# Sums of x begun in an earlier block, cached keys transposed later in half pairs, bias rows built beside the pair of values

## The chip, the cores and the metric

The kernel runs on one NeuronCore of a Trainium2 chip. The core has TensorE (PE, matrix multiply), VectorE (DVE), ScalarE (ACT), GpSimd (POOL) and SyncE (SP), which here only issues DMA transfers. Each engine works through its own instructions in the order in which they are written; an instruction waits until the semaphores it needs are set, and everything behind it on the same engine waits with it. TensorE writes to PSUM, and ACT and DVE copy the results from there to SBUF.

The metric is the device time of one execution in microseconds. Before the change the runs gave 1001.48, 997.56 and 995.86 us, a median of 997.56.

## The reference, cut to what matters

One layer of a streaming encoder runs on 1024 new prompt frames and 64 sample frames, with 512 cached frames for the samples.

```python
def project(x, norm_w, w_in, q_norm_w, k_norm_w):
    h = rms_norm(x, norm_w) @ w_in                      # (T, 1024) @ (1024, 6144)
    sb_q, sb_k, sb_v, sb_z, cb_q, cb_k, cb_v, cb_z, g_sb, g_cb = jnp.split(h, SPLIT_POINTS, axis=-1)
    ...
    cb_q = rms_norm(cb_q.reshape(lead + (N_HEADS_CB, HEAD_DIM)), q_norm_w)
    cb_k = rms_norm(cb_k.reshape(lead + (N_HEADS_CB, HEAD_DIM)), k_norm_w)
    ...
k_all = jnp.concatenate([cache_sb_k[l], sk2], axis=1)   # 512 cached keys + 64 new ones
o_sb2 = stick_breaking(sq2, k_all, v_all, s_qpos, sb_s_kpos)
kb = jnp.concatenate([cache_cb_k[l], ck2], axis=1)
o_cb2 = band_attention(cq2, kb, vb, s_qpos, cb_s_kpos, rel_bias[l])
```

The band attention adds a bias that depends on the clipped distance of query and key (`rel_bias`, 8 heads of 257 numbers). Then both branches are gated, projected, merged and added to x.

## The kernel before

Every float32 product is made of float32r parts: a value is split into a high part (ACT copies it, rounded) and a low part (value minus high part, on DVE or POOL), and hi·hi, lo·hi and hi·lo are summed in PSUM. On top of that stands a Strassen-like scheme with seven products in place of eight for the large projections; it needs sums of quarters of x and of quarters of the weights.

The order of the work on each engine is written out by hand: the program is emitted in loops, and what is emitted first is executed first on its engine. The stages that the change touches are these, in order:

- **Normalise and transpose x** (block 0 of the next loop carries it).
- **Plain blocks.** The loop over `i in range(nb)` with `nb = 6` (`NB = [1024, 1280, 2560, 2816, 2048, 2304]`) makes 256 columns of the projection for nine token tiles `ti` each. Blocks 0 and 1 are values of branch A and have no norm; blocks 2 and 3 are keys of branch B, blocks 4 and 5 its queries. In blocks 2 to 5 each tile needs a norm per head (`evac_nat`, `norm_nat`: a square on ACT, a reduction and two products on DVE, a power on POOL), and up to three tiles later `post_nat` transposes it on PE (tile `pk`, one PSUM buffer) and splits it (`hl`, L359 on ACT and L360 on DVE).
- Beside block 1 the cached keys are transposed: `cache_load` fetches a whole cache (`ck`, 1 MB), and `cache_pair` transposes 128 columns of it on PE into `pc`, splits them into `hc` (L379 on ACT, L380 on DVE; one buffer) and stores them to DRAM for the attention. The bias rows are built there too: `load_rb` fetches `rel_bias` to all partitions, `make_rb` negates and lays out a row for each head (`rx`, L249 and L250 on DVE) and stores it.
- Beside blocks 2 to 5 `make_t` forms the sums of x (`d`, L169 to L177 on DVE; `t0` to `t3`, ACT and L158 on DVE) in 17 pieces (`tjobs`), one at every second tile.
- **The pair of values** (`OPV`, L654 on PE) makes the values of branch B by the seven-product scheme.
- **The paired stage** (the loop over `pairs`, L832 on PE) makes 14 pairs of 128 columns, seven steps `s` each; a step is 24 matmuls. Step `n = 7*i + s` begins by preparing weights five steps ahead (`prep`, `presum`, `load_raw`), then `step()` emits what earlier steps left for later: stores of finished parts (`hl`) and, for key pairs, `out`, which transposes the part on PE (`kf`, `u`, `s` into `acc`, two PSUM buffers) and stores it (`ko`, `kos`). The first four pairs are keys and queries of branch A, and their stores are the most numerous.
- Attention, output projections and the last product follow; the change leaves them as they are.

Nearly all DMAs of these stages are issued by SP, in program order, stores and loads in one row. A store that waits for DVE holds the loads behind it.

Of the kernel before, what the change touches and what calls it, by code (L numbers as in the profile page):

```python
# [32 lines left out]
def hybrid_step_kernel(ctx: ExitStack, tc: tile.TileContext, x_prompt, x_sample, c_sbk, c_sbv, c_cbk, c_cbv,  # L33
# [15 lines left out]
    def rdma(out, in_):  # L49
        out, in_ = (a if isinstance(a, bass.AP) else a[:] for a in (out, in_))  # L50
        SP.dma_start(out.bitcast(F32), in_.bitcast(F32))
# [149 lines left out]
    with ExitStack() as ph:  # L201
# [37 lines left out]

        rbs = {}  # L240

        def load_rb():
            rbs[0] = p1.tile([128, 8, 257], F32, name="ck", bufs=3)
            SP.dma_start(rbs[0], rel_bias[0:1].to_broadcast([128, 8, 257]))

        def make_rb(h):
            rb = rbs[0]
            rx = p1.tile([128, 768], F32, name="rx", bufs=3)
            V.tensor_scalar(rx[:, 0:512], rb[:, h, 256:257].to_broadcast([128, 512]), -1.0, None, op0=OP.mult)  # L249
            V.tensor_scalar(rx[:, 512:768], rb[:, h, 255::-1], -1.0, None, op0=OP.mult)  # L250
            SP.dma_start(d_rb[h], rx)

        def rsqrt(dst, src, scale, n):
# [111 lines left out]
                    if t == 3:  # L365
                        rdma(dst[p0 + j][:, :, NP:T], h[:, j, :, 512:576])

        def cache_load(b):
            src = c_sbk if b == "sb" else c_cbk
            ck = p1.tile([128, 4, 512], F32, name="ck", bufs=3)  # L370
            SP.dma_start(ck, src.rearrange("(t p) c -> p t c", p=128))
            cks[b] = ck

        def cache_pair(b, p):
            pt = psK.tile([128, 4, 128], F32, name="pc")
            for t in range(4):
                TE.transpose(pt[:, t], cks[b][:, t, p * 128:(p + 1) * 128], ident)
            h = p1.tile([128, 2, 512], F32R, name="hc", bufs=1)
            A.activation(h[:, 0], pt[:].rearrange("p t c -> p (t c)"), AF.Copy)  # L379
            V.tensor_tensor(out=h[:, 1], in0=pt[:].rearrange("p t c -> p (t c)"), in1=h[:, 0].bitcast(F32),  # L380
                            op=OP.subtract)
            rdma(d_cT[b][p], h)

        raws, blk, sums = {}, {}, {}
        def load_raw(n):
            if n >= 2 * len(pairs):
# [32 lines left out]
        def prep(n):  # L419

            i, s = divmod(n, 7)
            if i >= len(pairs):
                return
            a, b = slice(0, 128), slice(128, 256)
            r1, r2 = raws[2 * i], raws[2 * i + 1] if s else None
            if s == 0:
                src = r1[:, :, a]
            elif s == 3:
                src = r2[:, :, a]
            elif s == 5:  # L430
# [8 lines left out]
            A.activation(t[:, 0], src, AF.Copy)  # L439
            G.tensor_tensor(out=t[:, 1], in0=src, in1=t[:, 0].bitcast(F32), op=OP.subtract)  # L440
            blk[n] = t
            if s == 6:
                load_raw(2 * i + 4)
# [44 lines left out]
        def v_sum(n):  # L488
            x, y, op, pool, name, bufs = {
                2: ((0, 1), (1, 1), OP.add, natx, "wlox", 2), 1: (2, (0, 0), OP.subtract, natx, "wlox", 2),  # L490
                4: ((0, 0), (0, 1), OP.subtract, natx, "whix", 2), 6: ((1, 0), 1, OP.subtract, None, "t6", 1)}[n]
            d = vraw[n] = (pool or pv2).tile([128, 4, 256], F32, name=name, bufs=bufs)
            V.tensor_tensor(out=d, in0=vraw[x], in1=vraw[y], op=op)

        def prep_v(q):
# [24 lines left out]
        for i in range(nb):  # L520
            for ti, t in enumerate(TO):
# [34 lines left out]
                if ti in (3, 6) and i > 0 or ti in (6, 7) and i == 0:  # L556
# [4 lines left out]
                        load_nat(i + 2, h)  # L561
                    else:
                        load_v_raw(*((0, 0), (1, 0), (0, 1), (1, 1))[2 * (i + 2 - nb) + h])
                if (i, ti) in ((0, 5), (0, 8)):
                    cache_load("sb" if ti == 5 else "cb")
                if i == 1 and ti < 8:
                    if ti == 0:
                        load_rb()
                    cache_pair("sb" if ti < 4 else "cb", ti % 4)
                if 10 <= 9 * i + ti < 18:  # L570
                    make_rb(9 * i + ti - 10)
                if (i, ti) == (1, 0):
                    psTx.close()
                if (i, ti) == (1, 8):
                    p1x.close()
                    tp = sx.enter_context(tc.tile_pool(name="tp", bufs=1))
                    pad(tp, 64)
                    tms = [[tp.tile([128, 4, HF], F32R, name=f"t{n}{s}") for s in "hl"] for n in range(4)]
                    tqx = ExitStack()
                    tq = tqx.enter_context(tc.tile_pool(name="tq", bufs=3))  # L580
                    tjobs = iter(make_t(tms, tq))
                if i > 1 and (i + ti) % 2:
                    next(tjobs, None)
                if (i, ti) == (nb - 1, 5):
                    prep_v(0)
                if (i, ti) == (nb - 1, 8):
                    v_sum(2)
                if (i, ti) in ((1, 1), (1, 5)):
                    for s in range(2):
                        h = ti // 4  # L590
# [39 lines left out]
        for q, s in enumerate(OPV):  # L630
# [14 lines left out]
            for c in range(2):  # L645
# [58 lines left out]

    with ExitStack() as ph:
        up = ph.enter_context(tc.tile_pool(name="a2u", bufs=3, side="right"))
        psB = ph.enter_context(tc.tile_pool(name="a2p", bufs=1, space=PS))
        LEAD, HB = 5, 4
        later = []

        def soon(n, f):
# [99 lines left out]
        for i in range(len(pairs)):  # L811
            bank, s1, u2, u3 = {}, {}, {}, {}
            for s in range(7):
# [941 lines left out]
```

## Time and profile before

| what | value |
|---|---|
| median of the three runs | 997.56 us |
| the profiled execution | 1000.77 us, of which the span is 999.0 us |
| PE busy | 964.0 us (96%) |
| DVE / ACT / POOL busy | 606.2 / 475.2 / 403.9 us |
| PE waits for DVE at the transposes of normed tiles (`pk`) | 14.9 us in 9 waits |
| PE waits for DVE at the transposes of cached keys (`pc`) | 10.6 us in 3 waits |
| plain block 1 | 42.78 to 84.84 us |
| plain blocks 2 to 5 | 84.84 to about 208 us |
| pair of values | about 208 to 257 us |
| paired stage | 257.56 to about 550 us |

The page's busy shares say which engine is the bound over the whole span. For a change that moves work between stages, a table by stage says more: the busy time of each engine in a stretch, the clock that TensorE was granted there (1.00 is full speed), and the DMA share. The list of waits tells who waited for whom; the rows of SP in order of time tell when a transfer was issued, and a row with `x3` is three instructions merged, its length from the first's start to the last's end, waits between them included.

### The profile page before, as it was taken

The page shows a single profiled execution, that of the slowest core. Times are in us where ns is not written, and L with a number is a line of the kernel's source. Part 1 is how long each engine was busy: PE and PEld are TensorE (multiplying, and loading weights), DVE is VectorE, ACT ScalarE, POOL GpSimd, SP SyncE. Part 2 cuts the span into 40 slices and gives each one's busy share as a digit, 9 for nine tenths or more (in the row PEclk, how much of TensorE's full clock was granted, in tenths as well). Part 3 has the DMA queues.
Part 4 walks back from the last instruction along what each step waited for, and adds up shares of the span by engine and source line. Part 5 has one row for each costly group of instructions (what it writes and reads, how often), then busy time and mean ns, then how long its engine had stood idle before and what let it go on. Part 6 is the DMA issues. An engine that isn't in the chain of part 4 may idle for free.

```text
span 999.0 us, 20386 instructions
## 1 busy us (share of the span) xinstructions
PE 964.0 (96%) x7591; PEld 915.0 (92%) x7591; DVE 606.2 (61%) x1185; ACT 475.2 (48%) x1046; POOL 403.9 (40%) x395
## 2 busy tenths in 40 slices
PE   8959789889999999999999999999999999999998
PEld 8959789889999999999999988788888889999998
DVE  6524899863545455553332267788668766389735
ACT  6513344342344343343333266677787776455220
POOL 3212665554545447655643211001341111596641
PEclk9989899999999999999999999999999999999999
DMA  6876234224565655556632697778799951862642
GB/s 220 264 253 238 81 103 148 98 93 134 164 178 160 199 163 182 163 162 190 186 109 78 186 278 209 204 200 233 213 265 268 247 152 56 249 209 81 200 137 84
DMA packets 173192, 175.76 MB, mean 176 GB/s; under 512 B 30553, under 2 KB 157405, under 8 KB 172966
## 3 DMA queue, kind: packets, MB, share of 16 engines
q1 hardware_dynamic: 161542, 159.45, 54.4%
q10 hardware_dynamic: 8736, 8.33, 2.6%
q0 software_dynamic: 2816, 6.69, 2.1%
q8 instruction: 60, 0.98, 0.4%
q14 instruction: 38, 0.31, 0.1%
HBM read 112.42 MB, written 62.00 MB: 175 GB/s over the span
## 4 chain that ended last, share of the span: by engine, by line
PE 82%; DVE 8%; DMA 4%; ACT 3%; issue 1%; POOL 1%; SPq 0%; ACTq 0%; DVEq 0%; POOLq 0%
PE b L832 29%; PE o L1349 7%; PE acc L519 7%; PE z L1257 7%; PE pt L1310 7%; PE b L1669 6%; PE acc L1108 5%; PE acc L1001 5%; PE b L1150 4%; PE v L654 3%; DMA d_csbT<-hc 2%; DVE qn L335 1%; DMA d_ccbT<-hc 1%; PE pt L283 1%; PE pk L355 1%
## 5 line engine op out<-in xcount | busy, mean ns | idle before, releaser
L1279 DVE TENSOR_TENSOR_SCAN be<-be,imp 128x128 f32<-128x128 f32 (+7 forms) x64 | 83.4, 1344 | 8.1 <-ACT be L1260 7.9
L1310 PE MATMUL pt<-ident,be 128*128 128x128 f32 (+1 forms) x568 | 87.7, 278 | 0.6 <-ACT wT L1319 0.2
L1257 PE MATMUL z<-ks,sq 128*128 128x320 f32 (+5 forms) x384 | 87.5, 338 | 0.0
L1310 PEld LDWEIGHTS pt<-ident,be 128*128 128x128 f32 (+1 forms) x568 | 65.7, 140 | 13.0 <-issue 4.6
L1319 ACT ACTIVATE wT<-pt 128x512 f32<-128x512 f32 (+3 forms) x123 | 57.0, 497 | 42.8 <-PE pt L1310 42.7
L840 DVE TENSOR_TENSOR u<-b,s 128x256 f32<-128x256 f32 (+1 forms) x56 | 24.1, 439 | 70.4 <-PE b L832 65.7
L1257 PEld LDWEIGHTS z<-ks,sq 128*128 128x128 f32 x384 | 63.6, 190 | 1.7
L1349 PE MATMUL o<-wT,vp 128*64 128x256 f32 (+1 forms) x608 | 64.2, 356 | 0.0
L1349 PEld LDWEIGHTS o<-wT,vp 128*64 128x64 f32 x608 | 40.3, 136 | 23.6 <-issue 7.5
L519 PE MATMUL acc<-whi,xa 128*128 128x256 f32 x192 | 55.6, 309 | 0.2 <-ACT xa L291 0.2
L1282 ACT ACTIVATE be<-be,sm 128x640 f32<-128x640 f32 (+5 forms) x68 | 47.2, 694 | 17.2 <-DVE sm L1281 17.1
L905 POOL DMA_DIRECT2D d_osb<-zt x20 | 10.8, 541 | 102.1 <-DVE zt L1358 63.2
L124 POOL TENSOR_TENSOR wlo<-wraw,whi 128x1024 fp32r<-128x1024 f32 x13 | 32.0, 2458 | 49.3 <-ACT whi L117 46.1
L519 PE MATMUL acc<-whi,xm 128*128 128x256 f32 x192 | 51.9, 290 | 0.0
L519 PE MATMUL acc<-wlo,xa 128*128 128x256 f32 x192 | 51.8, 289 | 0.0
L519 PE MATMUL acc<-whix,xm 128*128 128x256 f32 x192 | 50.6, 283 | 0.0
L519 PE MATMUL acc<-whix,xb 128*128 128x256 f32 x192 | 50.4, 282 | 0.0
L519 PE MATMUL acc<-wlox,xm 128*128 128x256 f32 x192 | 50.3, 282 | 0.0
L440 POOL TENSOR_TENSOR whix<-ws,whix 128x512 fp32r<-128x512 f32 x28 | 36.9, 1317 | 32.5 <-ACT whix L439 28.2
L1270 ACT ACTIVATE be<-be,sm 128x640 f32<-128x640 f32 (+5 forms) x68 | 47.3, 696 | 5.0 <-DVE sm L1262 4.5
L1260 ACT ACTIVATE be<-z 128x384 f32<-128x384 f32 (+6 forms) x104 | 47.9, 515 | 3.2 <-PE z L1257 2.4
L440 POOL TENSOR_TENSOR wlo<-ws,wlo 128x512 fp32r<-128x512 f32 x28 | 39.5, 1412 | 18.1 <-ACT wlo L439 17.9
(387 smaller groups left out, 3334.7 us busy)
## 6 DMA issues: line engine op xcount, KB each, us to landing
wraw<-in_w_in_dram SPq DMA_DIRECT2D x31, 512.0 KB, 4.1
wrawx<-in_w_in_dram SPq DMA_DIRECT2D x16, 512.0 KB, 4.8
sq<-d_qsbT SPq DMA_DIRECT2D x32, 192.0 KB, 6.1
sq<-d_qcbT SPq DMA_DIRECT2D x32, 192.0 KB, 5.2
xt<-in_x_prompt_dram SPq DMA_DIRECT2D x8, 512.0 KB, 6.5
d_kcbT<-hl SPq DMA_DIRECT2D x8, 512.0 KB
d_qcbT<-hl SPq DMA_DIRECT2D x8, 512.0 KB, 4.4
d_ksbT<-hl SPq DMA_DIRECT2D x16, 256.0 KB, 3.1
```

The costliest lines, as they stand in the source:

```text
L440: G.tensor_tensor(out=t[:, 1], in0=src, in1=t[:, 0].bitcast(F32), op=OP.subtract)
L519: TE.matmul(ps, x, w, start=first, stop=last)
L832: TE.matmul(ps[:, :m], w[:, hl_, k], right[s](x)[:, k, a:b], start=s < 3 and k == 0 and e == 0, stop=k == 3 and e == 2, skip_group_check=s ...
L1001: TE.matmul(ps[:, :b - a], w[:, k], xk(x, k)[:, a:b], start=k == 0 and n == 0, stop=k == KT - 1 and n == 2)
L1108: TE.matmul(ps[:, :e - a], w[:, p, cw], g[:, a:e], start=m % 12 == 0, stop=m % 12 == 11)
L1257: TE.matmul(z[:, :m], s[:, e, q0:q0 + 128], ks[:, h, o + x:o + y], start=(e, h) == parts[0], stop=(e, h) == parts[-1])
L1260: A.activation(be[:r, x:y], z[:r, :m], AF.Sigmoid, scale=-0.125)
L1279: V.tensor_tensor_scan(be[:r, n - 1::-1], be[:r, n - 1::-1], im[:, ::-1], 0.0, op0=OP.mult, op1=OP.max)
L1310: TE.transpose(pt[:kr, x, :r], be[:r, kb * 128:kb * 128 + kr], ident[:r, :r])
L1319: A.activation(w[:, sl:sl + m, q0:q0 + r], pt[:, :m, :r], AF.Copy)
L1349: TE.matmul(o[hd * 64:hd * 64 + 64, c0:c1], vv[:kr, kb, hd * 64:hd * 64 + 64], wT[b, p, j, hd, s // 4][:kr, s % 4, c0:c1] if j < 4 else wT ...
L1669: TE.matmul(ps[:, t], left[s](xs_, k)[:, ts_], wt_[:, k], start=s < 3 and t == k == e == 0, stop=k == 3 and e == 2, skip_group_check=s > 2 ...
```

## The change

Four things move.

1. `make_t` begins in block 1 instead of block 2: a piece at each tile from (1, 1) on, eight in block 1, and then one at every fourth tile instead of every second. The pool of block 0 is closed at (1, 0), and the copies of sample columns that the sums read are made at the end of block 0.
2. `cache_load` and `cache_pair` leave blocks 0 and 1. In the paired stage, steps 2 to 33, an even step loads a half pair (256 tokens by 128 columns, 128 KB, one buffer `ck`) and the odd step after it transposes it (two transposes into `acc`, split into `hc`, stored in the next `step()`): 16 loads and 16 parts.
3. The bias rows leave blocks 0 to 2: one row a head is loaded (`rb`) after product 2 of the pair of values, and `make_rb` is called beside products 3 to 5.
4. After the plain blocks the remaining `post_nat` are called one at a time in place of two, over products 0 to 2. `v_sum(6)` uses another buffer, and the low part of weight block 1 is made on DVE in place of POOL.

On DVE, at block 1, where a split of weights (L124) and the fold of the sample tile (L299) come first, the rows before are those of the cached keys and the bias rows:

```order
L124 TENSOR_TENSOR wlox<-wrawx,whix 128x1024
L299 TENSOR_TENSOR fl<-acc,fl 64x256
L380 TENSOR_TENSOR hc<-pc,hc 128x512
L596 TENSOR_SCALAR wqk<-wqk 128x64
L380 TENSOR_TENSOR hc<-pc,hc 128x512
L249 TENSOR_SCALAR rx<-ck 128x512
L250 TENSOR_SCALAR rx<-ck 128x256
```

The same place in the changed kernel, still on DVE:

```order
L124 TENSOR_TENSOR wlox<-wrawx,whix 128x1024
L299 TENSOR_TENSOR fl<-acc,fl 64x256
L572 TENSOR_SCALAR wqk<-wqk 128x64
L169 TENSOR_TENSOR d<-xa 128x544
L170 TENSOR_TENSOR d<-d,xm 128x544
L171 TENSOR_TENSOR d<-d,xm 128x544
L176 TENSOR_TENSOR d<-xm,d 128x544
L177 TENSOR_TENSOR d<-d,xb 128x544
L158 TENSOR_TENSOR t0l<-d,t0h 128x544
```

The sums of x stand where the cached keys and bias rows stood.

On SP, at the first key pair of the paired stage, before: raw weights (`wraw`, `wrawx`), stores of key parts (`hl`) and of the transposed outputs (`ko`, `kos`).

```order
L395 DMA wraw<-in_w_in_dram 128x4x256 x2
L51 DMA d_ksbT_70<-hl 256x1x256 x2
L51 DMA d_ksbT_70<-hl 256x1x32
L395 DMA wrawx<-in_w_in_dram 128x4x256
L764 DMA out_dram<-ko 128x2x128
L761 DMA out_dram<-kos 32x128
L764 DMA out_dram<-ko 128x2x128
L51 DMA d_ksbT_71<-hl 256x1x256 x2
L51 DMA d_ksbT_71<-hl 256x1x32
```

And SP at the same place after, with loads of half pairs (`ck`) and stores of the split keys (`hc`) between them:

```order
L379 DMA wraw<-in_w_in_dram 128x4x256 x2
L696 DMA ck<-in_cache_sb_k_dram 128x2x128
L51 DMA d_csbT_78<-hc 256x1x256
L51 DMA d_ksbT_70<-hl 256x1x256 x2
L51 DMA d_ksbT_70<-hl 256x1x32
L696 DMA ck<-in_cache_sb_k_dram 128x2x128
L379 DMA wrawx<-in_w_in_dram 128x4x256
L763 DMA out_dram<-ko 128x2x128
L760 DMA out_dram<-kos 32x128
L763 DMA out_dram<-ko 128x2x128
L51 DMA d_ksbT_71<-hl 256x1x256 x2
L51 DMA d_ksbT_71<-hl 256x1x32
```

Each load of a half pair stands behind the stores that its step emits.

On PE, at the end of step 4 and the begin of step 5 of the paired stage (`t2` and `t3` are sums of x, `kf` a finished key part), before:

```order
L832 MATMUL b_3332<-t2l,whix 128x288
L832 MATMUL b_3332<-t2h,whix 128x288
L756 MATMUL acc<-ident,kf 128x128 x4
L758 MATMUL acc<-ident,kf 32x128
L832 MATMUL b_3317<-t3h,whi 128x256
```

And PE there after:

```order
L833 MATMUL b_3273<-t2l,whix 128x288
L833 MATMUL b_3273<-t2h,whix 128x288
L755 MATMUL acc<-ident,kf 128x128 x4
L757 MATMUL acc<-ident,kf 32x128
L702 MATMUL acc<-ident,ck 128x128 x2
L833 MATMUL b_3258<-t3h,whi 128x256
```

Two transposes of a half pair now stand ahead of the step's matmuls.

The diff, cut to its core:

```diff
-        def load_rb():
-            rbs[0] = p1.tile([128, 8, 257], F32, name="ck", bufs=3)
-            SP.dma_start(rbs[0], rel_bias[0:1].to_broadcast([128, 8, 257]))
+        def load_rb(h):
+            rbs[h] = pv2.tile([128, 257], F32, name="rb", bufs=3)
+            SP.dma_start(rbs[h], rel_bias[0:1, h:h + 1].to_broadcast([128, 1, 257]).rearrange("p o n -> p (o n)"))
 
         def make_rb(h):
-            rb = rbs[0]
-            rx = p1.tile([128, 768], F32, name="rx", bufs=3)
...
+            rb = rbs.pop(h)
+            rx = pv2.tile([128, 768], F32, name="rx", bufs=2)
...
-        def cache_load(b):
...
-        def cache_pair(b, p):
...
-            G.tensor_tensor(out=t[:, 1], in0=src, in1=t[:, 0].bitcast(F32), op=OP.subtract)
+            (V if n == 1 else G).tensor_tensor(out=t[:, 1], in0=src, in1=t[:, 0].bitcast(F32), op=OP.subtract)
...
-                if (i, ti) in ((0, 5), (0, 8)):
-                    cache_load("sb" if ti == 5 else "cb")
-                if i == 1 and ti < 8:
-                    if ti == 0:
-                        load_rb()
-                    cache_pair("sb" if ti < 4 else "cb", ti % 4)
-                if 10 <= 9 * i + ti < 18:
-                    make_rb(9 * i + ti - 10)
                 if (i, ti) == (1, 0):
                     psTx.close()
-                if (i, ti) == (1, 8):
+                if (i, ti) == (1, 0):
                     p1x.close()
...
                     tjobs = iter(make_t(tms, tq))
-                if i > 1 and (i + ti) % 2:
+                elif i == 1 or i > 1 and (9 * i + ti) % 4 == 0:
                     next(tjobs, None)
...
-                if (i, ti) in ((1, 1), (1, 5)):
+                if (i, ti) in ((0, 7), (0, 8)):
...
-                if q < 2:
-                    for _ in range(2):
-                        if pend and (q or c):
-                            post_nat(*pend.pop(0))
+                if q < 3 and pend and (q or c):
+                    post_nat(*pend.pop(0))
+                for h in {(3, 0): (0,), (3, 1): (1, 2), (4, 0): (3,), (4, 1): (4, 5), (5, 0): (6,), (5, 1): (7,)}.get((q, c), ()):
+                    make_rb(h)
+                    if h + 3 < 8:
+                        load_rb(h + 3)
...
-            if q == 1:
+            if q == 2:
                 assert not pend
...
             if q == 2:
+                for h in range(3):
+                    load_rb(h)
                 v_sum(4)
...
+        cjobs = [(b, p, h) for b in ("sb", "cb") for p in range(NPAIR) for h in range(2)]
+        cks = {}
+
+        def cache_load(b, p, h):
+            cks[b, p, h] = cq.tile([128, 2, 128], F32, name="ck")
+            src = (c_sbk if b == "sb" else c_cbk)[256 * h:256 * h + 256, p * 128:(p + 1) * 128]
+            SP.dma_start(cks[b, p, h], src.rearrange("(t p) c -> p t c", p=128))
+
+        def cache_part(b, p, h):
+            ck = cks.pop((b, p, h))
+            pt = psF.tile([128, 512], F32, name="acc")[:, 0:256]
+            for t in range(2):
+                TE.transpose(pt[:, t * 128:(t + 1) * 128], ck[:, t], ident)
+            hc = cq.tile([128, 2, 256], F32R, name="hc")
+            A.activation(hc[:, 0], pt, AF.Copy)
+            V.tensor_tensor(out=hc[:, 1], in0=pt, in1=hc[:, 0].bitcast(F32), op=OP.subtract)
+            soon(0, lambda: rdma(d_cT[b][p][:, :, 256 * h:256 * h + 256], hc))
...
                 step()
+                if 2 <= n < 2 + 2 * len(cjobs):
+                    (cache_part if n % 2 else cache_load)(*cjobs[(n - 2) // 2])
```

More of the change, by code (lines that the diff above doesn't have):

```diff
@@ L240, in hybrid_step_kernel @@
         rbs = {}
-        def load_rb():
-            rbs[0] = p1.tile([128, 8, 257], F32, name="ck", bufs=3)
-            SP.dma_start(rbs[0], rel_bias[0:1].to_broadcast([128, 8, 257]))
+        def load_rb(h):
+            rbs[h] = pv2.tile([128, 257], F32, name="rb", bufs=3)
+            SP.dma_start(rbs[h], rel_bias[0:1, h:h + 1].to_broadcast([128, 1, 257]).rearrange("p o n -> p (o n)"))
         def make_rb(h):
-            rb = rbs[0]
-            rx = p1.tile([128, 768], F32, name="rx", bufs=3)
-            V.tensor_scalar(rx[:, 0:512], rb[:, h, 256:257].to_broadcast([128, 512]), -1.0, None, op0=OP.mult)
-            V.tensor_scalar(rx[:, 512:768], rb[:, h, 255::-1], -1.0, None, op0=OP.mult)
+            rb = rbs.pop(h)
+            rx = pv2.tile([128, 768], F32, name="rx", bufs=2)
+            V.tensor_scalar(rx[:, 0:512], rb[:, 256:257].to_broadcast([128, 512]), -1.0, None, op0=OP.mult)
+            V.tensor_scalar(rx[:, 512:768], rb[:, 255::-1], -1.0, None, op0=OP.mult)
             SP.dma_start(d_rb[h], rx)
@@ L366, in post_nat @@
                         rdma(dst[p0 + j][:, :, NP:T], h[:, j, :, 512:576])
-        def cache_load(b):
[L369 to L372, printed above, removed]
-        def cache_pair(b, p):
[L375 to L382, printed above, removed]
         raws, blk, sums = {}, {}, {}
@@ L490, in v_sum @@
                 2: ((0, 1), (1, 1), OP.add, natx, "wlox", 2), 1: (2, (0, 0), OP.subtract, natx, "wlox", 2),
-                4: ((0, 0), (0, 1), OP.subtract, natx, "whix", 2), 6: ((1, 0), 1, OP.subtract, None, "t6", 1)}[n]
-            d = vraw[n] = (pool or pv2).tile([128, 4, 256], F32, name=name, bufs=bufs)
+                4: ((0, 0), (0, 1), OP.subtract, natx, "whix", 2), 6: ((1, 0), 1, OP.subtract, natx, "wlox", 2)}[n]
+            d = vraw[n] = pool.tile([128, 4, 256], F32, name=name, bufs=bufs)
             V.tensor_tensor(out=d, in0=vraw[x], in1=vraw[y], op=op)
@@ L587, in hybrid_step_kernel @@
                     v_sum(2)
-                if (i, ti) in ((1, 1), (1, 5)):
+                if (i, ti) in ((0, 7), (0, 8)):
                     for s in range(2):
-                        h = ti // 4
+                        h = ti - 7
                         for c in range(2):
@@ L706, in hybrid_step_kernel @@
         up = ph.enter_context(tc.tile_pool(name="a2u", bufs=3, side="right"))
+        cq = ph.enter_context(tc.tile_pool(name="cq", bufs=1))
         psB = ph.enter_context(tc.tile_pool(name="a2p", bufs=1, space=PS))
         LEAD, HB = 5, 4
+        cjobs = [(b, p, h) for b in ("sb", "cb") for p in range(NPAIR) for h in range(2)]
[13 more added lines that the diff above has]
+            soon(0, lambda: rdma(d_cT[b][p][:, :, 256 * h:256 * h + 256], hc))
         later = []
```

## The prediction

> **What bounds the kernel now.** I read the page's busy shares first, then a table by stage.
>
> ```profile
> PE 964.0 (96%) x7591; PEld 915.0 (92%) x7591; DVE 606.2 (61%) x1185; ACT 475.2 (48%) x1046; POOL 403.9 (40%) x395
> ```
> ```profile
> 42.78:84.84 42.06, 31.46 (x242) 30.86 (x241) 9.97 (x22) 9.73 (x19) 5.99 (x6) 0.88 0.74 251
> 84.84:116.44 31.60, 27.93 (x220) 27.54 (x219) 20.95 (x40) 11.12 (x28) 15.63 (x17) 0.89 0.33 119
> 116.44:148.07 31.63, 27.16 (x229) 26.16 (x228) 29.20 (x55) 12.94 (x34) 18.57 (x20) 1.00 0.39 127
> 148.07:177.08 29.01, 28.23 (x228) 27.76 (x228) 26.77 (x53) 13.46 (x35) 18.50 (x20) 0.94 0.42 142
> 177.08:208.20 31.12, 28.34 (x230) 27.93 (x228) 27.00 (x53) 11.98 (x33) 16.90 (x21) 0.95 0.32 106
> 208.20:224.60 16.40, 13.19 (x99) 12.71 (x97) 8.67 (x14) 6.05 (x12) 7.70 (x6) 0.90 0.26 89
> ...
> 257.56:299.14 41.58, 41.58 (x332) 41.04 (x333) 21.25 (x40) 17.94 (x45) 23.25 (x16) 1.00 0.57 171
> ```
>
> The columns are stretch, length, busy time of PE, PE's weight loads, DVE, ACT and POOL, then granted clock, DMA share and GB/s. The first five stretches are plain blocks 1 to 5, the sixth the begin of the pair of values. PE idles there, and its clock is not full. In blocks 3 to 5 DVE is busy 92, 92 and 87%. In the paired stage (last row) PE has no gap and full clock: whatever is put on its path there is paid in full. The waits and the chain of waits say who holds PE in the plain blocks:
>
> ```profile
> PE pk L355 <- DVE hl L360: 14.9, 9, 3.7
> PE pc L377 <- DVE hc L380: 10.6, 3, 7.8
> ```
> ```profile
> 48.88 8.85 DMA d_csbT<-hc
> 57.83 0.61 ACT hc L379
> 58.46 0.70 DVE hc L380
> 59.18 2.64 DMA d_csbT<-hc
> ...
> 110.77 2.74 PE acc L519 x24
> ...
> 113.51 0.23 PE pk L355 x2
> ```
>
> In block 1 the one `hc` buffer makes a chain: store, ACT, DVE, store. In blocks 2 to 5 DVE is late for `pk`. A tile of 24 matmuls without a wait takes 2.74 us (0.114 each), two transposes 0.23.
>
> The clock follows the gaps. The bracket is PE's idle time before the row:
>
> ```profile
> 120.15 0.44 PE L355 MATMUL pk<-ident,qn 128*128 128x128 f32 x2 [1.58 <-DVE hl L360]
> ```
> ```profile
> 147.88 0.47 PE L355 MATMUL pk<-ident,qn 128*128 128x128 f32 x2 [1.95 <-DVE hl L360]
> ```
> ```profile
> 120.35:123.30 2.95, 2.95 (x29) 2.95 (x28) 2.12 (x7) 2.04 (x5) 1.63 (x3) 1.00 0.67 228
> 148.15:151.57 3.42, 3.42 (x19) 3.42 (x18) 3.18 (x8) 1.48 (x4) 3.08 (x4) 0.50 0.74 259
> ```
>
> After the gap of 1.95 us PE ran at half clock for 3.4 us (19 matmuls where the full clock gives 30); after 1.58 us it did not. So a gap of about 2 us costs itself and 3.42 × 0.5 = 1.7 us more.
>
> **The change part by part.**
>
> *Plain block 1* has 208 matmuls: 208 × 0.114 = 23.8 us against 42.06, so 18.3 us go if nothing new holds it. New there are eight pieces of the sums: 20 additions and seven splits on DVE.
>
> ```profile
> L177 DVE TENSOR_TENSOR d<-d,xb 128x544 f32<-128x544 f32 x8 | 5.8, 725 | 0.3
> ```
>
> 27 × 0.725 = 19.6 us (a split is as wide as an addition), less than the block's 23.8, and PE needs DVE there only for the sample tile's fold. That is the cover; the gain falls if DVE carries a backlog into block 2.
>
> *Plain blocks 2 to 5* take 31.60 + 31.63 + 29.01 + 31.12 = 123.4 us. Unhindered they are 4 × 23.8 and 32 pairs of transposes at 0.23, 102.6: at most 20.8 us. Their DVE load falls from 103.9 us by 19.6 to 84.3, 82% of 102.6. A piece at every fourth tile still puts two to four additions and splits ahead of a tile's own work, so I take 17, with 21 and 4 as ends.
>
> *Begin of the pair of values*: two `post_nat` in one place make the second wait for DVE; its gaps are 16.40 − 13.19 = 3.2 us and its clock 0.90 (another 1.6). One at a time: 4.5 of 4.8.
>
> *Bias rows*: a row has 768 columns, two thirds of them in the 0.42 us below, so eight times some 0.65 us on DVE beside products 3 to 5.
>
> ```profile
> L249 DVE TENSOR_SCALAR rx<-ck x8: 417/419/1221, 59.1 to 90.0; 128x512 f32<-128x512 f32 x8
> ```
> ```profile
> 225.00:250.00 25.00, 25.00 (x222) 25.00 (x221) 7.53 (x10) 6.48 (x8) 11.84 (x5) 1.00 0.43 137
> ```
>
> DVE is idle 17 of 25 us there, so I cost them at nothing; if a row's load were late, DVE would hold an evacuation, which PE misses only a product later (48 × 0.114 = 5.5 us). The other buffer of `v_sum(6)`: nothing.
>
> Gain: 18.3 + 17 + 4.5 = 39.8.
>
> *Transposes of cached keys*: the 32 stay, now on the path at 0.23 a pair: 16 × 0.23 = +3.7.
>
> *Their loads* are the dear part. PE takes a part at the begin of an odd step, one step (24 matmuls, 2.99 us) after its load is issued at best. But SP comes to that load only behind the stores of its step, and they wait for DVE:
>
> ```profile
> 259.40 7.69 SPq L395 DMA_DIRECT2D wraw<-in_w_in_dram  x2
> 269.12 2.86 SPq L51 DMA_DIRECT2D d_ksbT<-hl  x3
> 276.53 0.38 SPq L395 DMA_DIRECT2D wrawx<-in_w_in_dram  x1
> ...
> 283.28 2.09 SPq L51 DMA_DIRECT2D d_ksbT<-hl  x3
> ...
> 326.78 2.61 SPq L51 DMA_DIRECT2D d_ksbT<-hl  x3
> ```
> ```profile
> 300.63 1.91 SPq L51 DMA_DIRECT2D d_qsbT<-hl  x3
> ```
> ```profile
> 344.93 1.91 SPq L51 DMA_DIRECT2D d_qsbT<-hl  x3
> ```
> ```profile
> 266.67 0.28 PE L832 MATMUL b<-xm,wlox 128*128 128x256 f32 x1
> ```
> ```profile
> 272.63 0.60 PE L756 MATMUL acc<-ident,kf 128*128 128x128 f32 x4
> ```
> ```profile
> 280.02 0.60 PE L756 MATMUL acc<-ident,s 128*128 128x128 f32 x4
> ```
> ```profile
> 299.14 0.28 PE L832 MATMUL b<-xm,wlo 128*128 128x256 f32 x1
> ```
> ```profile
> 324.92 0.37 PE L832 MATMUL b<-xa,whi 128*128 128x256 f32 x1
> 343.43 0.28 PE L832 MATMUL b<-xm,wlo 128*128 128x256 f32 x1
> ```
> ```profile
> wraw<-in_w_in_dram SPq DMA_DIRECT2D x11, 512.0 KB, 4.0
> ...
> out_dram<-ko SPq DMA_DIRECT2D x16, 128.0 KB, 4.1
> ...
> dva<-d_sbv SPq DMA_DIRECT2D x7, 128.0 KB, 2.7
> ```
> ```profile
> L440 POOL TENSOR_TENSOR whix<-ws,whix 128x512 fp32r<-128x512 f32 x28 | 36.9, 1317 | 32.5 <-ACT whix L439 28.2
> ```
>
> No half-pair load is in the trace. Its landing is bounded by `dva` (a load of 128 KB, 2.7 us from issue) and `ko` (128 KB, 4.1); I take 2.7, the like kind, and 3.5 where a raw weight block is ahead of it. A store of `hc` ahead of it costs SP 0.6, a third of 1.91. Then, in the times of before:
>
> - Part 1 (step 3, PE at 266.67): its load follows the raw load whose issue ends at 267.09; the split that moved to DVE frees it 1.3 us earlier (one split on POOL, the last row), the raw block lands 4.0 later and the half pair just behind it, near 269.7: a wait of 3.0.
> - Parts 2 and 3: part 3's load stands behind the stores that SP ends at 285.37; SP has issued one DMA after the other from 276.53 on, once DVE let the raw load go. 285.37 + 0.6 + 2.7 = 288.7; PE is there at 280.02 + 0.44 (the finished part's own transposes) = 280.5. The two parts lose 8.2 together, however it falls between them.
> - Part 6 (step 13): 302.54 + 0.6 + 3.5 = 306.6 against 299.14: 7.5.
> - Part 7: its load follows three stores of the step before, as at 269.12, which end 2.3 after the step's begin (269.64, one step before 272.63), here 0.5 later for one more addition; 2.8 + 2.7 against 2.99: 2.5.
> - Second key and query pair: parts 9 and 10, 329.39 + 0.6 + 2.7 = 332.7 against 324.92: 7.8. Part 13, 346.84 + 0.6 + 3.5 = 350.9 against 343.43: 7.5.
> - Part 14 as part 7: 2.5; part 16 as part 2 alone: 2.0. The other six find their loads landed.
>
> Sum: 3.0 + 8.2 + 7.5 + 2.5 + 7.8 + 7.5 + 2.5 + 2.0 = 41.0. Seven of these gaps are 2 us or more and bring half clock: 7 × 1.7 = 12. Behind the waiting transposes stand PE's matmuls, nothing that could run instead.
>
> [...]
>
> **Sum**: −39.8 + 3.7 + 41.0 + 12 = +16.9. The profiled execution took 1000.77 us (span 999.0), so 1017.7; the median of the runs is 3.2 lower, so 997.56 + 16.9 = 1014.5.
>
> **The rivals.** What a measurement of this kernel tells from no change is about 0.5%, 5 us.
>
> *A, faster: the loads keep ahead.* While PE waits once, SP works off its row, and the next loads may be issued in time. Waits and clock together must stay under 39.8 − 3.7 − 5 = 31 us in place of 53. If only parts 1 to 3 and 6 wait, 18.7 and 5, the sum is −12: 985; with none, 961. For it: SP is not full over a pair, only late. Against: in steps 4 to 6 the stores wait for results of the step just before, and no earlier wait changes that.
>
> *B, no change*: waits and clock of 31 to 41 us, as when parts 3, 6, 10 and 13 wait no longer than part 7.
>
> *C, slower still: DVE keeps holding PE in blocks 2 to 5.* With a gain there of 4 in place of 17 the time is 1027.5. For it: block 5 at 87% DVE has gaps of 2.8 us and block 4 at 92% only 0.8, so the load alone does not set them. Against: half of the pieces are gone, and with them half of the places where a tile comes late.
>
> **Numbers.** The forecast has 0.59, A 0.18, B 0.08, C 0.15. So faster 0.18, same 0.08, slower 0.74. The forecast's own range is 1000 to 1024: up by landings of 4.1 for all eight terms (six times 1.4, twice 0.6: 9.6), down by a gain of 21 in blocks 2 to 5 (4) and no waits at parts 7, 14 and 16 (7, and 3.4 of clock). The range that holds 8 in 10 goes down to A at 985, and up to C with those landings, 1037.
>
> **What would show it.** PE's idle time before `acc<-ident,ck` of some 40 us in 16, ended by the load of `ck`, with half clock behind it; SP's load rows late in steps 4, 6 and 12 of a pair of pairs; plain block 1 near 24 us and blocks 2 to 5 near 26 each, with few waits at `pk`. If the waits at `ck` come to under 20 us, the forecast is wrong by A; if blocks 2 to 5 stay near 31, by C.

## The result, and the profile after

The changed kernel takes 1035.61 us (median of four runs, 1034.92 to 1036.22), the kernel before 997.98 us in the same session (995.86 to 1001.48): a ratio of 1.0373 with an interval of 1.0343 to 1.0404. The forecast was 1014.5. The profiled execution of the changed kernel took 1035.35 us, with a span of 1033.6 against 999.0: 34.6 us more, 17.7 more than the forecast's sum of 16.9. (The medians lie 37.6 us apart; the profiled execution of the kernel before was 2.8 us above its median.)

First the busy shares on the page of the changed kernel:

```profile
PE 973.5 (94%) x7591; PEld 924.4 (89%) x7591; DVE 607.0 (59%) x1194; ACT 478.8 (46%) x1054; POOL 400.6 (39%) x394
```

PE has the same 7591 matmuls as before. Its busy time is 9.5 us longer, 8.1 of it because more of the work ran at half clock (39.1 us of its busy time, 22.9 before), and its idle time grew from 35 to 60 us. Where both lie is told by the table by stage (stretch, length, busy time of PE, its weight loads, DVE, ACT and POOL, then granted clock, DMA share, GB/s). The rows are plain blocks 1 to 5, the pair of values, and the paired stage:

```profile
43.05:67.13 24.08, 24.08 (x210) 24.08 (x209) 17.54 (x22) 8.63 (x17) 5.34 (x4) 1.00 0.43 128
67.13:94.58 27.45, 25.38 (x220) 24.79 (x219) 23.81 (x41) 11.32 (x28) 15.77 (x16) 1.00 0.22 66
94.58:121.03 26.45, 26.45 (x229) 26.25 (x228) 21.39 (x46) 11.86 (x32) 17.91 (x20) 1.00 0.45 146
121.03:148.73 27.70, 26.68 (x230) 26.13 (x228) 21.95 (x45) 11.87 (x32) 19.48 (x22) 1.00 0.47 153
148.73:175.24 26.51, 26.51 (x229) 26.31 (x228) 20.89 (x46) 11.46 (x32) 16.71 (x21) 1.00 0.38 125
175.24:229.30 54.06, 47.07 (x379) 46.31 (x378) 28.11 (x44) 13.87 (x23) 20.08 (x11) 0.94 0.58 193
229.30:591.83 362.53, 319.63 (x2425) 316.55 (x2426) 140.69 (x280) 122.21 (x278) 155.26 (x127) 0.94 0.49 148
```

Plain block 1 has no gap and full clock now, and blocks 2 to 5 have 3.1 us of gaps and full clock. The last two rows have lost what the others gained: PE idles 7.0 us in the pair of values and 42.9 us in the paired stage, and the clock is 0.94 in both. Before, these stages took 49.4 us (208.19 to 257.56) and 297.7 us (257.56 to 555.26), the latter without a gap and at full clock.

Set against the forecast's own terms (the clock lost is half of PE's busy time at half clock, added up by stage):

| stage | before | after | difference | forecast |
|---|---|---|---|---|
| plain block 1 | 42.1 | 24.1 | −18.0 | −18.3 |
| plain blocks 2 to 5 | 123.4 | 108.1 | −15.2 | −17 |
| pair of values | 49.4 | 54.1 | +4.7 | −4.5 |
| paired stage: PE's gaps | 0 | 42.9 | +42.9 | +41.0 |
| paired stage: half clock | 0 | 16.6 | +16.6 | +12 |
| paired stage: transposes and the rest | | | +5.3 | +3.7 |
| all other work | | | −1.7 | 0 |
| sum | | | +34.6 | +16.9 |

The list of waits of PE in the changed kernel names what ends the gaps (total, times, longest):

```profile
PE acc L702 <- DMA ck<-in_cache_sb_k_dram: 18.7, 4, 7.8
PE acc L702 <- DMA ck<-in_cache_cb_k_dram: 18.0, 5, 7.9
PE acc L702 <- ACT ko L761: 6.1, 4, 2.9
...
PE pk L355 <- DVE hl L360: 3.1, 3, 1.6
PE v L630 <- ACT whi L483: 2.5, 1, 2.5
PE v L630 <- POOL wlo L484: 1.9, 1, 1.9
PE v L630 <- DVE u L645: 1.6, 1, 1.6
```

18.7 + 18.0 + 6.1 = 42.8 us stand before the transposes of half pairs (L702), 36.7 of them ended by the load of `ck`. The other 6.1 are not waits for a load: finished keys were transposed into both `acc` buffers just before, and PE waits until ACT has copied one of them out (`ko`), 2.9 us each at parts 2 and 9. The waits at `pk` have fallen from 14.9 to 3.1 us. The last three rows are new, and belong to the pair of values.

How a half-pair load comes late is seen at part 6, the longest gap of the first key and query pair. SP's rows (start, length), then DVE, then PE (the bracket is the idle time before the row), all of the changed kernel:

```profile
281.50 2.84 SPq L51 DMA_DIRECT2D d_qsbT<-hl  x3
289.15 0.39 SPq L379 DMA_DIRECT2D wraw<-in_w_in_dram  x1
289.63 0.52 SPq L51 DMA_DIRECT2D d_csbT<-hc  x1
290.24 2.16 SPq L51 DMA_DIRECT2D d_qsbT<-hl  x3
292.50 1.03 SPq L696 DMA_DIRECT2D ck<-in_cache_sb_k_dram  x1
```
```profile
288.40 0.69 DVE L391 TENSOR_TENSOR ws<-wraw 128x512 f32<-128x512 f32 x1
```
```profile
296.17 0.66 PE L702 MATMUL acc<-ident,ck 128*128 128x128 f32 x2 [7.76 <-DMA ck<-in_cache_sb_k_dram]
```

SP stands from 284.34 to 289.15 at the next load of weights, whose buffer `wraw` DVE lets go at 289.09, and has five more DMAs to issue before it comes to the half pair at 292.50. PE ended the step's matmuls at 288.4 and waits until 296.17: the load landed 3.7 us after its issue.

### The profile page after: what moved, and what is told of

It reads as the page before. It is cut to its first block, busy times and chain, and to the rows that moved or that the text cites. A ratio compares the mean times of both kernels' runs of the same rounds, so it can differ in the third digit from the quotient of the medians.

```text
span 1033.6 us, 20473 instructions
## 1 busy us (share of the span) xinstructions
PE 973.5 (94%) x7591; PEld 924.4 (89%) x7591; DVE 607.0 (59%) x1194; ACT 478.8 (46%) x1054; POOL 400.6 (39%) x394
## 4 chain that ended last, share of the span: by engine, by line
PE 64%; DMA 1%; SPq 1%; ACT 1%; issue 1%; DVE 0%; ACTq 0%
PE b L833 22%; PE b L1670 7%; PE o L1350 7%; PE z L1258 7%; PE pt L1311 6%; PE acc L1109 5%; PE b L1151 5%; PE acc L1002 5%; DMA ck<-in_cache_cb_k_dram 1%; PE acc L1706 1%; SPq L51 0%; PE acc L702 0%; SPq L778 0%; ACT wT L1320 0%; PE b L1706 0%
## 5 line engine op out<-in xcount | busy, mean ns | idle before, releaser
L1320 ACT ACTIVATE wT<-pt 128x512 f32<-128x512 f32 (+3 forms) x123 | 56.9, 495 | 42.8 <-PE pt L1311 42.7
L424 POOL TENSOR_TENSOR wlo<-ws,wlo 128x512 fp32r<-128x512 f32 x27 | 36.3, 1346 | 44.4 <-ACT wlo L423 43.5
L503 PE MATMUL acc<-whi,xa 128*128 128x256 f32 x192 | 52.5, 293 | 0.2 <-ACT xa L291 0.2
L503 PE MATMUL acc<-whi,xm 128*128 128x256 f32 x192 | 49.8, 279 | 0.0
L702 PE MATMUL acc<-ident,ck 128*128 128x128 f32 x32 | 8.1, 342 | 42.9 <-DMA ck<-in_cache_sb_k_dram 18.7
```

What stands on the lines that cost most here:

```text
L424: (V if n == 1 else G).tensor_tensor(out=t[:, 1], in0=src, in1=t[:, 0].bitcast(F32), op=OP.subtract)
L503: TE.matmul(ps, x, w, start=first, stop=last)
L1320: A.activation(w[:, sl:sl + m, q0:q0 + r], pt[:, :m, :r], AF.Copy)
```

## The experiments

**The theory**: the half-pair loads are late because SP takes its row in order, and a load that is to be used one step later is reached only behind the stores and loads ahead of it, up to 7 us late. What decides is the number of steps between a load and its use. **The rival**: SP or the DMA has too much to do in these steps, so that fewer loads in a stretch, or another issuing engine, would be the cure at one step's distance too.

**One load in four steps, taken three steps later.** The changed kernel loads at every even step and takes at the step after it. Here the 16 parts are spread over 64 steps, with the load three steps ahead, still on SP and still with one buffer:

```diff
-                if 2 <= n < 2 + 2 * len(cjobs):
-                    (cache_part if n % 2 else cache_load)(*cjobs[(n - 2) // 2])
+                j, o = divmod(n - 2, 4)
+                if 0 <= j < len(cjobs) and o in (0, 3):
+                    (cache_part if o else cache_load)(*cjobs[j])
```

> One job of the cached keys every four steps (steps 2 to 65), its load three steps ahead of its part; the load stays on SP. Theory (the load is issued late in SP's row, and one step is too short for that): the longest time from the begin of the loading step to the landing in the changed kernel is about 10.9 us (a wait of 7.9 after a step of 3.0), three steps are 9, so PE's waits for ck fall from 36.7 us to under 6, the half-clock loss from 16 to under 4, and the time to 985 to 995. Rival (the transfers themselves are slow, or PE waits for PSUM held by ACT): waits of 25 us or more stay, and the time is over 1015.

It takes 991.70 us (991.08 to 993.57), a ratio to the kernel before of 0.994 (0.9925 to 0.9955). Its waits of PE and its paired stage:

```profile
PE acc L702 <- ACT ko L761: 7.4, 3, 4.4
...
PE acc L702 <- DMA ck<-in_cache_sb_k_dram: 3.4, 2, 1.9
...
PE acc L702 <- DMA ck<-in_cache_cb_k_dram: 1.9, 2, 1.1
```
```profile
228.40:547.88 319.48, 306.66 (x2425) 304.30 (x2426) 140.35 (x280) 121.10 (x278) 156.60 (x127) 0.99 0.55 168
```

The waits for `ck` fall from 36.7 to 5.3 us, and the clock lost in the stage from 16.6 to 3.3, as the theory had it. The waits for `ko` stay, at 7.4 us, so they do not come from late loads. With the same transposes and the same loads on the same queue the kernel now takes 0.6% less than the one before, a small gain but clear of the noise. But two things were changed at once, the spacing and the distance; the next two runs keep the spacing.

**The same spacing, taken one step later** (`o in (0, 1)`), **and two steps later** (`o in (0, 2)`).

> The same spread over steps 2 to 65, but the load one step ahead as in the changed kernel. Theory of the late issue: the wait belongs to the kind of step that loads (long where a raw load or stores of the step stand ahead), so the sum stays at 30 to 45 us and the time at 1022 to 1037. Rival (SP is simply too full in the first four pairs, and half the jobs in the later, lighter pairs are free): waits under 25 us and a time under 1018.

> One job every four steps as in the two runs before it, the load two steps ahead. Theory of the late issue: the time from step to landing is set by SP's row and not by PE, so each wait of the run with one step (60.8 us for ck) shrinks by one step, 3.0 us, and no further: about 27 us for ck are left, with 8 to 15 us of half clock, and the time is 1008 to 1022, between the 991.7 of three steps and the 1064.1 of one. Rival (there is a threshold, a load just has to be issued before the step's stores): under 1000.

At one step 1064.13 us (1062.5 to 1065.91), ratio 1.0663 (1.0647 to 1.068); at two 1021.6 us (1017.42 to 1028.38), ratio 1.023 (1.0181 to 1.028). The waits of PE, of the run at one step's distance and of the run at two:

```profile
PE acc L702 <- DMA ck<-in_cache_sb_k_dram: 33.7, 6, 7.3
PE acc L702 <- DMA ck<-in_cache_cb_k_dram: 27.1, 7, 6.3
```
```profile
PE acc L702 <- DMA ck<-in_cache_sb_k_dram: 14.4, 5, 5.0
PE acc L702 <- DMA ck<-in_cache_cb_k_dram: 12.9, 5, 3.7
```

| load to use | waits for `ck` | all gaps of the paired stage | clock lost there | paired stage | time |
|---|---|---|---|---|---|
| 1 step, every 2nd step (the change) | 36.7 | 42.9 | 16.6 | 362.5 | 1035.6 |
| 1 step, every 4th step | 60.8 | 63.8 | 22.4 | 388.1 | 1064.1 |
| 2 steps, every 4th step | 27.3 | 29.8 | 12.3 | 344.6 | 1021.6 |
| 3 steps, every 4th step | 5.3 | 12.8 | 3.3 | 319.5 | 991.7 |

At equal spacing each further step takes 22 to 34 us of waits away, and the run at two steps came out as the theory had it, in the waits (27.3 us) and in the time. Half as many loads in a stretch do not help by themselves: they make it worse, against the rival and also against my figure for this run, which was 27 us too low at its upper end. 13 of the 16 parts wait for their load there, against 9 with the closer spacing. The closer spacing is cheaper, as I read the two traces, because while PE waits at one part SP works off its row, and a next load two steps on finds it short; with four steps between, the row is late again each time. That reading was not tested by itself. Slow landings have a small part in the waits of the changed kernel: PE went on 2.4 to 3.7 us after the issue of the load that it waited for began, and only once later, at 6.6 us.

**The loads on POOL's queue.** One word changes: `G.dma_start` for `SP.dma_start` at the load of the half pair, at the distance of one step.

> The changed kernel with the 16 loads of half pairs issued by POOL in place of SP, at the same places of the program, one step ahead. Theory of the late issue in SP's row: POOL waits for no store, so the loads are issued early in their step, waits for ck fall from 36.7 to under 12 us and the time to 995 to 1012. Rival (the landing is what takes long): waits stay over 25 us and the time over 1020.

It takes 1041.95 us (1041.56 to 1042.28), ratio 1.0441 (1.0425 to 1.0456), with 38.9 us of waits for `ck`. By the letter these are the rival's numbers, but the rows of POOL and PE at part 6 show why:

```profile
291.73 1.62 POOL L424 TENSOR_TENSOR wlox<-wrawx,wlox 128x512 fp32r<-128x512 f32 x1 [4.04 <-ACT wlox L423]
293.30 0.72 POOL L696 DMA_DIRECT2D ck<-in_cache_sb_k_dram  x1
```
```profile
297.66 0.66 PE L702 MATMUL acc<-ident,ck 128*128 128x128 f32 x2 [6.10 <-DMA ck<-in_cache_sb_k_dram]
```

POOL was 39% busy in the changed kernel, yet it too takes its work in order: the load stands behind a split of weights that waited 4.04 us for ACT. The load went from one row that waits to another. It also took longer to land, 4.4 us from the begin of its issue where the changed kernel's load at part 6 took 3.7. So this run does not tell the two apart; the runs on distance do.

**One bias row built instead of eight.** The pair of values was forecast 4.5 us shorter and became 4.7 us longer. The rows suspected are those of DVE there, in the changed kernel:

```profile
200.80 1.00 DVE L249 TENSOR_SCALAR rx<-rb 128x512 f32<-128x512 f32 x1 [2.10 <-DMA rb<-in_rel_bias_dram]
...
206.99 0.43 DVE L249 TENSOR_SCALAR rx<-rb 128x512 f32<-128x512 f32 x1 [1.67 <-DMA d_rb<-rx]
...
214.77 0.43 DVE L249 TENSOR_SCALAR rx<-rb 128x512 f32<-128x512 f32 x1 [2.81 <-DMA d_rb<-rx]
...
215.31 1.22 DVE L477 TENSOR_TENSOR wlox<-wraw,wlox 128x1024 f32<-128x1024 f32 x1
```

DVE waits for the load of a row, and then again and again for the store of an earlier row, since `rx` has two buffers. Behind the wait of 2.81 us stands the weight sum for the last product (`wlox`, L477), and behind that ACT and POOL, which split it:

```profile
216.64 1.06 ACT L483 ACTIVATE whi<-wlox 128x1024 fp32r<-128x1024 f32 x1 [15.13 <-DVE wlox L477]
```
```profile
217.78 2.34 POOL L484 TENSOR_TENSOR wlo<-wlox,whi 128x1024 fp32r<-128x1024 f32 x1 [13.74 <-ACT whi L483]
```
```profile
217.75 0.39 PE L630 MATMUL v<-whi,xm 128*128 128x256 f32 x1 [2.55 <-ACT whi L483]
220.17 0.58 PE L630 MATMUL v<-wlo,xm 128*128 128x256 f32 x1 [1.92 <-POOL wlo L484]
```

In this run the first row is built, and stored for all eight heads; the loads and stores stay, the other seven rows are not built:

```diff
+        one = []
+
         def make_rb(h):
             rb = rbs.pop(h)
+            if one:
+                SP.dma_start(d_rb[h], one[0])
+                return
             rx = pv2.tile([128, 768], F32, name="rx", bufs=2)
...
+            one.append(rx)
```

> The changed kernel with one bias row built and stored for all eight heads: the seven other rows are not built, so every head gets the bias of the first; the loads and the eight stores stay. Theory (DVE waits for the two row buffers to be stored, and holds the weight sum and the evacuations of the pair of values): PE's waits at that stage (2.5 for ACT, 1.9 for POOL, 1.6 for DVE) and the half clock after them go, the time falls by 7 to 10 us to about 1027. Rival (the pool that is closed one product later, or the stores on SP): no change, 1033 or more.

1029.31 us (1028.28 to 1031.14), 6.3 less than the changed kernel, where I had written 7 to 10. Its pair of values:

```profile
175.28:221.51 46.23, 43.77 (x379) 43.40 (x378) 22.36 (x29) 13.87 (x23) 20.10 (x11) 1.00 0.61 208
```

46.23 us for 54.06, at full clock: the two waits for the splits are gone, only the 1.6 us of the first row stay. All eight loads and stores are there, so the transfers by themselves are not the cost; it is what the seven other rows put into DVE's row. Ahead of the weight sum that is 1.67 + 0.52 + 2.81 = 5.0 us of waits for stores and some 3.5 us of work on five rows. The run does not separate the two.

**The sums of x as before.** The pieces of the sums are put back to every second tile of blocks 2 to 5, none in block 1; the cached keys stay in the paired stage.

```diff
-                elif i == 1 or i > 1 and (9 * i + ti) % 4 == 0:
+                if i > 1 and (i + ti) % 2:
                     next(tjobs, None)
```

> The changed kernel with one part undone: the 17 pieces of the sums of x again at every second tile of blocks 2 to 5, none in block 1; cached keys and bias rows stay where the change put them. Theory (blocks 2 to 5 are shorter because half of the pieces are gone from them): these blocks grow from 107.9 us to 118 to 124, and the time to 1045 to 1052. Rival (they are shorter because block 1 hands DVE over without a backlog of cached keys and bias rows): they stay under 113 us and the time under 1041.

1046.1 us (1043.01 to 1048.91), ratio 1.0468 (1.0438 to 1.0499). Blocks 2 to 5 of this run:

```profile
67.14:92.89 25.75, 25.25 (x220) 24.86 (x219) 19.08 (x35) 10.64 (x27) 15.68 (x16) 1.00 0.23 69
92.89:125.11 32.22, 27.45 (x230) 26.43 (x228) 29.68 (x55) 12.95 (x34) 19.08 (x21) 1.00 0.39 125
125.11:154.15 29.04, 28.35 (x229) 27.95 (x228) 26.77 (x53) 13.48 (x35) 18.51 (x20) 0.94 0.43 142
154.15:185.21 31.06, 28.30 (x230) 27.88 (x228) 26.92 (x53) 12.01 (x33) 16.88 (x21) 0.95 0.32 107
```

Together 118.1 us, between 108.1 after the change and 123.4 before. So the moved sums are worth 10 of the 15.2 us in these blocks. The other 5 come with the cached keys and bias rows gone from block 1: block 2 alone falls from 31.60 to 25.75 us here. DVE's fold of the sample tile of block 1 (`fl`, L299) shows why, before the change and in this run:

```profile
90.56 0.41 DVE L299 TENSOR_TENSOR fl<-acc,fl 64x256 f32<-64x256 f32 x1
```
```profile
69.57 0.42 DVE L299 TENSOR_TENSOR fl<-acc,fl 64x256 f32<-64x256 f32 x1 [23.50 <-ACT fl L298]
```

Before, DVE came to it 5.7 us into block 2 (from 84.84 on), straight from a cached key and two bias rows of block 1; here it comes 2.4 us in (from 67.14 on), after idling. Blocks 3 to 5 are as they were before the change (31.63, 29.01 and 31.12 there).

**Both causes removed.** The loads three steps ahead as in the first run, and the bias rows out of the pair of values into the paired stage, one in four steps: a row loaded at one step, built three steps later in two tiles of 256 columns, and stored with the stores of the step after. In one kernel the cached keys come first (steps 2 to 65) and the rows behind them (66 to 97); in the other the rows come first (2 to 33) and the keys behind (34 to 97). The core of the second:

```diff
-            rx = pv2.tile([128, 768], F32, name="rx", bufs=2)
-            V.tensor_scalar(rx[:, 0:512], rb[:, 256:257].to_broadcast([128, 512]), -1.0, None, op0=OP.mult)
-            V.tensor_scalar(rx[:, 512:768], rb[:, 255::-1], -1.0, None, op0=OP.mult)
-            SP.dma_start(d_rb[h], rx)
+            far, near = (pools[0].tile([128, 256], F32, name=x, bufs=1) for x in ("rf", "rn"))
+            V.tensor_scalar(far, rb[:, 256:257].to_broadcast([128, 256]), -1.0, None, op0=OP.mult)
+            V.tensor_scalar(near, rb[:, 255::-1], -1.0, None, op0=OP.mult)
+
+            def put():
+                for x, src in ((0, far), (256, far), (512, near)):
+                    SP.dma_start(d_rb[h][:, x:x + 256], src)
+            pools[1](0, put)
...
-                if 2 <= n < 2 + 2 * len(cjobs):
-                    (cache_part if n % 2 else cache_load)(*cjobs[(n - 2) // 2])
...
+                j, o = divmod(n - 34, 4)
+                if 0 <= j < len(cjobs) and o in (0, 3):
+                    (cache_part if o else cache_load)(*cjobs[j])
+                j, o = divmod(n - 2, 4)
+                if 0 <= j < 8 and o in (0, 3):
+                    (make_rb if o else load_rb)(j)
```

> The version with loads three steps ahead (cached keys in steps 2 to 65), and the bias rows moved out of the pair of values into steps 66 to 97 of the paired stage, each row built from two tiles of 256 columns three steps after its load. Theory (the rows cost 6 to 9 us beside the pair of values because DVE waits for their loads and stores there): 982 to 986 against 991.7. Rival (the end of the plain blocks or the later closing of the pool costs it): 990 or more.

> As the version before, in the other order: bias rows in steps 2 to 33, cached keys in steps 34 to 97, where no finished keys are transposed into the same PSUM buffers. Theory (ACT's late copies of finished keys hold those buffers: 7.4 us of waits in three gaps and some 5 us of half clock): 972 to 979. Rival (rows in the busy key pairs make DVE wait for their late loads): 985 or more.

Keys first: 985.89 us (984.94 to 989.15), ratio 0.9871 (0.9839 to 0.9903). Rows first: 975.95 us (973.78 to 977.73), ratio 0.9766 (0.9741 to 0.979), faster than both kernels. The pair of values and the paired stage of the latter, and its waits of PE:

```profile
175.24:219.58 44.34, 43.47 (x379) 43.30 (x378) 19.57 (x28) 13.87 (x23) 20.06 (x11) 1.00 0.43 140
219.58:531.97 312.39, 305.40 (x2425) 302.53 (x2426) 153.50 (x296) 120.20 (x278) 157.13 (x127) 0.99 0.61 185
```
```profile
PE acc L701 <- DMA d_dv<-dva: 2.8, 1, 2.8
PE acc L701 <- DMA ck<-in_cache_sb_k_dram: 2.6, 3, 1.0
```

Without the rows the pair of values takes 44.34 us in both kernels: 5.0 less than before the change, near the 4.5 that I had forecast for `post_nat` one at a time (which no run tests alone), and 9.7 less than in the changed kernel, which is what the bias rows cost there. With the keys from step 34 on, the transposes no longer meet the waits that ACT's evacuation of `ko` ends (7.3 us in the kernel with the keys first, none here). The waits for `ck` come to 2.6 us in place of 6.8, or to 5.4 with the 2.8 us at part 1, which the list puts down to the store of `dva`: part 1 reads nothing of `dva`, and that it waited for its own load is my reading.

## Where the prediction was right, and where it failed

The sign and the main mechanism held; the size did not. The medians lie 37.6 us apart where 16.9 were forecast, and 1035.6 us is outside the forecast's own range of 1000 to 1024. That it is inside the wider range, up to 1037, is luck: that end stood for rival C and slow landings, neither of which came. By the forecast's steps:

- **Plain block 1**, −18.3 forecast, −18.0 measured: it runs at PE's pace, and DVE's 17.5 busy us of 24.1 cover the sums, as the sum of 19.6 under 23.8 said.
- **Plain blocks 2 to 5**, −17 forecast, −15.2 measured. A third of it is another mechanism than I gave: block 2 is freed of the cached keys and bias rows of block 1 that DVE had still to work off there.
- **Waits for half pairs**, 41.0 forecast, 42.9 measured, part by part: part 1 3.6 (forecast 3.0); parts 2 and 3 together 7.5 (8.2); part 6 7.8 (7.5); part 7 2.7 (2.5); 9 and 10 together 7.6 (7.8); 13 7.9 (7.5); 14 2.5 (2.5); 16 1.3 (2.0); the others 2.0 (0). The landings of 2.7 and 3.5 us, taken from `dva` and the raw blocks, were 2.4 to 2.8 and 3.6 to 3.7 where PE waited, but for one of 6.6 at part 15, which I had as landed. The runs on distance show that the late issue is the cause of the 36.7 us that loads ended. The other 6.1, at parts 2 and 9 above all, are waits for ACT's copy of finished keys, which the forecast does not have; that the sum came so near in spite of it is in part luck.
- **Half clock**, 12 forecast, 16.6 measured: a term that was mis-sized. I counted parts 2 and 3, and 9 and 10, as one gap each; they are two gaps with a step between, so nine gaps and not seven bring half clock, and two of them, those of 7.8 and 7.9 us, lose some 2.4 us each in place of 1.7. Seven times 1.7 and twice 2.4 are the 16.6, but for rounding. (By my own limit, gaps of 2 us or more, part 16 with its 2.0 should have been counted as well; it came to 1.3 and brought none.)
- **Begin of the pair of values**, −4.5 forecast: −5.0 by the two runs that take the rows elsewhere, so right in size.
- **Bias rows: the step that failed.** "DVE is idle 17 of 25 us there, so I cost them at nothing" was wrong by 9.7 us, 54.06 against 44.34 with the rows elsewhere; 6.1 of them are gaps of PE and 2.9 half clock. The price that I named for a late row, an evacuation held and missed a product later (5.5 us), looked at the wrong thing. What DVE held back was the weight sum of the last product, which ACT must split and then POOL before PE can go on; and what made DVE late was less the load than the store of the row two before, which I had not counted as a wait at all. The idle time of DVE was a mean over 25 us. While DVE waits for a transfer it is idle too, as for 2.81 us ahead of the weight sum, but what stands behind in its row is held.

Of the rivals, A (the loads keep ahead) is refuted: 42.9 + 16.6 us against the 31 that it allows. So are B, for the same reason, and C, since DVE holds PE for 3.1 us in blocks 2 to 5. But C's principle came true one stage later. The miss of 17.7 us is 9.2 in the stage of the bias rows, 4.6 of half clock in the paired stage, and smaller terms.

## What to carry to other kernels

Issue a load as many steps ahead as its engine's row can be late, not only as long as it takes to land. Here the half pair of part 6 took 3.7 us from its issue to its use, but it stood behind a row that was held for 4.8 us, and PE waited 7.8 us; with one load in four steps PE waited 60.8, 27.3 and 5.3 us at one, two and three steps' distance. Another engine's row was no cure: POOL's, which waited 4.04 us ahead of the same load, left 38.9 us of waits. Before work is costed at nothing because its engine is idle, look for the transfers that it waits for, loads and the stores that free its buffers, and follow what is queued behind it down to PE. Here the same work, with the loads three steps ahead, one in four steps, and the bias rows out of the pair of values, turned +3.7% into −2.3%.

## What the runs showed of the hardware

From half clock after a gap of 1.95 us and none after 1.58 us I had taken a limit on the length of a gap, and a price of 1.7 us for each gap beyond it. The changed kernel around part 6, and around a gap of 1.58 us at part 15, and the kernel before around its gap of 1.95 us (third column PE's busy time, granted clock third from the end; the stretch behind the last one shown is the row of 148.15 in the prediction, at half clock):

```profile
287.49:290.91 3.42, 0.92 (x7) 0.68 (x6) 2.32 (x6) 1.38 (x3) 1.62 (x1) 1.00 0.15 26
290.91:294.32 3.41, 0.00 (x0) 0.00 (x0) 0.46 (x1) 0.96 (x2) 1.26 (x1) 0.50 1.05 346
294.32:297.74 3.42, 1.57 (x8) 1.60 (x9) 0.41 (x1) 0.38 (x1) 0.00 (x0) 0.50 0.73 223
297.74:301.15 3.41, 3.41 (x17) 3.41 (x17) 0.87 (x3) 0.42 (x1) 0.00 (x0) 0.50 0.22 77
301.15:304.56 3.41, 3.41 (x29) 3.41 (x28) 1.52 (x3) 1.26 (x3) 1.11 (x1) 1.00 0.23 78
```
```profile
386.49:389.90 3.41, 1.83 (x16) 1.63 (x15) 0.34 (x1) 0.90 (x3) 1.27 (x1) 1.00 0.07 20
389.90:393.31 3.41, 3.41 (x30) 3.41 (x29) 0.96 (x3) 2.25 (x4) 0.23 (x1) 1.00 0.34 115
```
```profile
144.74:148.15 3.41, 1.46 (x14) 1.26 (x12) 3.41 (x5) 0.00 (x0) 1.53 (x1) 1.00 0.17 41
```

At part 6 the clock is half for 10.24 us (290.91 to 301.15), of which PE works 5.0 us: the gap of 7.8 us loses 2.5 us more. All gaps of 1.9 us or more in the traces of the two kernels, from 20 us after the start to 8 us before the end, with the half clock that began in them or behind them (us):

| kernel | gaps of PE | half clock, for each | of it PE busy |
|---|---|---|---|
| before | 1.95, 2.01, 2.78 | 3.41 | 3.41 |
| before | 2.58 | 3.41 | 3.03 |
| before | 3.67 | 6.83 | 6.04 |
| before | 7.84 | 6.83 | 3.62 |
| after | 2.53, 2.65, 2.88, 2.88, 3.64 | 3.41 | 3.30 to 3.41 |
| after | 4.66, 4.74 | 3.41 | 3.28, 3.26 |
| after | 7.76, 7.92 | 10.24 | 4.98, 4.78 |
| after | 2.55 and, 0.5 us later, 1.92 | 6.83, for both | 5.89 |

The other gaps there, the longest of 1.65 us, brought no half clock. The one price does not hold: a gap of 3.67 us lost 3.0 us of clock in the kernel before, one of 4.74 us lost 1.6 in the changed kernel, and gaps of 7.84 and 7.76 us were followed by 6.83 and 10.24 us of half clock. So in these traces the length of a gap alone does not tell its cost; what else decides, no run shows.
